# A conv and RWKV7 trunk step: the order planned by a detailed timing model, and solved columns transposed on chip

## The chip, the cores and the metric

One core of one Trainium2 chip runs the whole program. Its engines work side by side, each through its own instruction stream in a fixed order: TensorE (PE, matrix products into PSUM), VectorE (DVE), ScalarE (ACT), GpSimd (POOL) and SyncE (SP, which here only issues DMAs). An instruction waits in its stream until what it needs is there, and everything behind it on that engine waits with it. The metric is device time in microseconds for one launch; the kernel before was run three times, and its median counts.

## The reference, cut to what matters

A layer of width 1024 over one prompt of 2048 positions and 8 short samples. All columns are one projection of the normalised input, half of them go to a short convolution, half to an RWKV-7 recurrence of 8 heads of 64, and the concatenated results go through an output projection:

```python
p = xn @ w_in
u = cg * h;  z = conv_w[0]*u_ext[:, 0:T] + conv_w[1]*u_ext[:, 1:T+1] + conv_w[2]*u_ext[:, 2:T+2]
y_conv = bg * z * silu(gc)
# recurrence, per head:
sa = einsum('bhij,bhj->bhi', S, -kk_t)
S  = S * w_t + sa (kk_t a_t)^T + v_t k_t^T
o  = einsum('bhij,bhj->bhi', S, r_t)
y  = concatenate([y_conv, group_norm(o) ... * silu(gr)]) @ w_out
out = rms_norm(x + y)
```

## The kernel before

**Tiling.** The prompt is worked in two halves (hf) of 1024 positions, and each half in four pairs of heads (p), so there are eight passes, pairs 0 to 7. A half has three blocks of columns, 256 (330 with the samples in the first half), 384 and 384 wide. Every projection is a sum over 8 pieces of the depth and three products of high and low parts (xh*wh, xl*wh, xh*wl), 24 matmuls into one PSUM tile `pj`; of these there are two buffers.

**One pass.** `rwkv_pair` projects k, r, v and the gate of the pair and, block by block, makes the decays and the small matrices: `amat` multiplies `L` by `bk` into PSUM tiles `ax` (four or three chunks, two heads), DVE masks the result into `AB` and `L`, POOL scales `AB` by `Q`. When a block is done, `store_blocks` writes the two 32x32 diagonal blocks of every chunk's triangular matrix to DRAM (`dn`). `inverse` (L640) reads them back as `na`, one small matrix to a partition, and solves: `subst` takes 31 steps of two DVE operations each, `sub<-xi,na` and `xi<-xi,sub`. Its result `xi` has one small matrix to a partition; the matmuls that follow (`cx`, 32x32) need the matrix over 32 partitions, so `xi` goes to DRAM (`dx`, two DMAs, L669) and comes back in another order (twelve DMAs into `AB`, L678), and DVE transposes one copy into `na` (L680) for a product. After the `cx` products `AB` holds the full inverse.

`wkv` then carries the state through 16 chunks of 64 positions, strictly one after the other. A chunk of the two heads is twelve fp32 matmul instructions of 64 columns, and a chain runs through them: `ca<-sv,L` (PE), the copy `xs` (DVE, L741), `ca<-xs,AB` (PE), `u` (DVE, L751), `cb<-u,bt` (PE), and two scalar_tensor_tensor operations that make the next state `sv` (DVE, L120), from which the next chunk's `ca` starts. `oo` (the output) and `cb<-sv,bt` stand beside the chain. Projections of the next pair and of the convolution (`conv_group`) don't depend on it, and can stand between its links on PE.

At the end `out_weights` and 17 output tiles of 512-column projections follow.

**What sets the order.** The loops are written as above, pass by pass, but instructions aren't issued in that order: the framework's scheduler, inside `tile.TileContext` (L1020 of before), plans an order for each engine ahead of time, from the dependencies, the buffers and the times that it estimates. That order is fixed in the program. SP issues nearly all loads and stores in one queue of this kind.

Of the kernel before, what the change touches and what calls it, by code (L numbers as in the profile page):

```python
# [8 lines left out]
F32 = mybir.dt.float32  # L9
# [4 lines left out]
ALU = mybir.AluOpType  # L14
# [73 lines left out]
def trunk_kernel(ctx, tc, I, O):  # L88
    nc = tc.nc
# [9 lines left out]
    def T(pool, shape, tag, bufs=1, dt=F32):  # L99
        cnt[0] += 1  # L100
        return pools[pool].tile(shape, dt, tag=tag, bufs=bufs, name=f"{tag}_{cnt[0]}")
# [71 lines left out]
    pool.memset(ucarry, 0.0)  # L173

    def derive():
        dve.tensor_scalar(out=omm, in0=prm[:, P_MU:P_MU + 17], scalar1=-1.0, scalar2=1.0, op0=ALU.mult, op1=ALU.add)
        dve.tensor_scalar(out=nkk, in0=prm[:, P_KK:P_KK + 4], scalar1=-1.0, scalar2=None, op0=ALU.mult)
# [462 lines left out]
    def inverse(S):  # L640
# [5 lines left out]
        for q in range(2):  # L646
            pool.memset(xf[q * 64:q * 64 + 64, q::34], 1.0)
        for q in range(2):
            sync.dma_start(out=na[q * 64:q * 64 + 64], in_=S.dn.rearrange("h b c s t -> (h b c) s t"))
        if cb:  # L650
# [14 lines left out]
        yield  # L665
        cnt[0] += 1
        dx = dram.tile([2, 2, 16, 16, 2, 32], F32, tag="dx", bufs=2, name=f"dx_{cnt[0]}")
        for q in range(2):
            sync.dma_start(out=dx[:, :, :, :, q, :].rearrange("h b c s t -> (h b c) s t"), in_=x[q * 64:q * 64 + 64])  # L669
        ty = T("pair", [128, 2, 16, 32], "na", 1)  # L670
        t1, ys = ty[:, 0], ty[:, 1]
        for bl in S.bls:
            AB, n, c0_ = S.AB[bl.i], bl.nch, bl.ch0
            e = 1 if bl.samp else 0
            for h in range(2):
                for b in range(2):
                    r = h * 64 + b * 32
                    sync.dma_start(out=AB[r:r + 32, e:e + n, b * 32:b * 32 + 32],  # L678
                                   in_=dx[h, b, c0_:c0_ + n].rearrange("c s q t -> (s q) c t"))
            dve.transpose(out=t1[:, c0_:c0_ + n, :], in_=AB[:, e:e + n, 0:32])  # L680
            py = CX([128, n, 32])
            for c in range(n):
                for h in range(2):
                    a, b = h * 64, h * 64 + 32
                    mm(py[b:b + 32, c, :], AB[a:a + 32, e + c, 32:64], t1[a:a + 32, c0_ + c, :])
            copy(ys[32:64, c0_:c0_ + n], py[32:64])
# [342 lines left out]
```

## Time and profile before

| | before |
|---|---|
| median of three runs | 1621.16 us (1619.57 to 1629.75) |
| profiled execution, its own time | 1613.0 us |
| span in the profile | 1610.9 us |
| PE busy | 1512.1 us, 94% |
| DVE busy | 1011.3 us, 63% |
| ACT busy | 616.2 us, 38% |
| POOL busy | 289.6 us, 18% |
| mean granted clock of TensorE | 0.969 |

The span is the time from the first to the last instruction of the profiled execution, and its own time has what lies around it. Busy shares are averages over stages that differ: PE is full in some stretches and has holes in others, so the page is read first for who could be the bound, and the stretches are then looked at one by one. The granted clock is 1.00 at 2.4 GHz and 0.50 at 1.2 GHz; a mean between them says how long each held.

### The profile page before, as it was taken

To read this page: it belongs to the slowest core of one execution; us is meant where nothing else is said; L and a number is where in the kernel's file an instruction comes from. 1 tells how busy PE (TensorE), PEld (TensorE's weight loads), DVE (VectorE), ACT (ScalarE), POOL (GpSimd) and SP (SyncE) were. 2 spreads that over 40 slices of the span, in tenths; PEclk is the share of its full clock that TensorE was granted. 3 is DMA by queue.
4 is the path that set the end of the run, shared out by engine and by line. 5 is a ranking of instruction groups with operands and counts; after the bars stand their busy time and mean duration, and the time that the engine had idled before them with its cause. 6 is when DMAs were issued, how large, how long until landed. Compare 5 with 4: busy or idle time off the path is not lost.

```text
span 1610.9 us, 29335 instructions
## 1 busy us (share of the span) xinstructions
PE 1512.1 (94%) x11088; PEld 1265.4 (79%) x11088; DVE 1011.3 (63%) x3101; ACT 616.2 (38%) x1591; POOL 289.6 (18%) x395
## 2 busy tenths in 40 slices
PE   4999999999999999989999999999999999899997
PEld 4989778887788777877789678877897788567885
DVE  6377458765687458784586358545864578466544
ACT  6443346324542354344541354135313543342221
POOL 3134103311133112320022002200220022000000
PEclk9989999899999998999999899999999999899999
DMA  7323412342043213441124112411241145414441
GB/s 241 118 83 110 137 49 74 108 122 78 20 136 113 95 50 112 140 125 61 36 73 125 42 36 66 135 39 37 77 127 38 34 118 155 133 62 137 143 137 53
DMA packets 121967, 151.90 MB, mean 94 GB/s; under 512 B 62617, under 2 KB 86681, under 8 KB 121826
## 3 DMA queue, kind: packets, MB, share of 16 engines
q1 hardware_dynamic: 107024, 104.53, 21.2%
q0 software_dynamic: 9536, 34.64, 6.8%
q10 hardware_dynamic: 5266, 10.86, 1.9%
q8 instruction: 88, 1.44, 0.4%
q14 instruction: 53, 0.43, 0.1%
HBM read 92.60 MB, written 57.35 MB: 93 GB/s over the span
## 4 chain that ended last, share of the span: by engine, by line
PE 63%; DVE 23%; issue 5%; DMA 5%; ACT 2%; POOL 1%; SPq 1%; ACTq 0%; DVEq 0%; POOLq 0%
PE pj L129 41%; PE ca L129 5%; PE ax L129 5%; DVE sub L123 5%; PE cb L129 4%; DVE xi L123 4%; DVE hp L123 2%; PE oo L129 2%; PE cx L129 2%; DVE hp L120 1%; PE cx L703 1%; DVE bk L123 1%; DVE t L120 1%; DMA dx<-xi 1%; DMA AB<-dx 1%
## 5 line engine op out<-in xcount | busy, mean ns | idle before, releaser
L129 PE MATMUL pj<-xh,wh 128*128 128x384 f32 (+3 forms) x1856 | 655.4, 354 | 18.0 <-DVE hp L123 13.8
L129 PE MATMUL pj<-xl,wh 128*128 128x384 f32 (+3 forms) x1856 | 652.8, 352 | 2.7 <-POOL xl L207 2.1
L129 PE MATMUL pj<-xh,wl 128*128 128x384 f32 (+3 forms) x1856 | 650.9, 351 | 0.8 <-DMA wl<-wsp 0.8
L129 PEld LDWEIGHTS pj<-xh,wh 128*128 128x128 f32 x1856 | 356.7, 192 | 50.1 <-DVE hp L123 11.5
L129 PEld LDWEIGHTS pj<-xl,wh 128*128 128x128 f32 x1856 | 356.8, 192 | 31.7 <-POOL xl L207 3.0
L129 PEld LDWEIGHTS pj<-xh,wl 128*128 128x128 f32 x1856 | 355.8, 192 | 27.3 <-issue 1.7
L117 ACT ACTIVATE tS<-sv,wc 64x64 f32<-64x64 f32 x256 | 88.0, 344 | 114.8 <-DVE sv L120 94.2
L207 POOL TENSOR_TENSOR wl<-wr,wh 128x512 fp32r<-128x512 f32 x66 | 87.8, 1342 | 193.4 <-ACT wh L117 190.0
L120 DVE SCALAR_TENSOR_TENSOR sv<-cb,wc,tS 64x64 f32<-64x64 f32 x240 | 68.0, 283 | 62.6 <-PE cb L129 56.1
L129 PE MATMUL ax<-L,bk 64*128 64x128 f32 x528 | 79.1, 298 | 20.9 <-DVE bk L123 11.2
L129 PEld LDWEIGHTS ax<-L,bk 64*128 64x128 f32 x528 | 66.1, 197 | 37.9 <-issue 23.6
L123 DVE TENSOR_TENSOR sub<-xi,na 128x126 f32<-128x126 f32 (+22 forms) x248 | 81.5, 329 | 16.5 <-DMA na<-dn 9.7
L117 ACT ACTIVATE t<-pj,prm 128x384 f32<-128x384 f32 (+3 forms) x170 | 68.8, 433 | 54.5 <-PE pj L129 53.4
L751 DVE TENSOR_SCALAR u<-ca,Q 128x64 f32<-128x64 f32 x128 | 36.2, 283 | 82.3 <-PE ca L129 82.1
L531 POOL TENSOR_TENSOR bk<-t,t 64x384 f32<-64x384 f32 (+2 forms) x56 | 58.3, 1041 | 155.3 <-ACT t L503 72.9
L123 DVE TENSOR_TENSOR xi<-xi,sub 128x126 f32<-128x126 f32 (+22 forms) x248 | 77.6, 313 | 7.1
L117 ACT ACTIVATE wh<-wr 128x512 fp32r<-128x512 f32 x66 | 40.5, 626 | 92.0 <-PE pj L129 73.1
L129 PEld LDWEIGHTS ca<-sv,L 128*64 128x64 f32 x528 | 43.3, 134 | 37.2 <-DVE sv L120 12.8
L129 PE MATMUL ca<-sv,L 128*64 128x64 f32 x528 | 67.8, 245 | 0.1
L741 DVE COPY xs<-ca 128x64 f32<-128x64 f32 x128 | 28.7, 224 | 60.4 <-PE ca L129 50.6
L298 POOL DMA_DIRECT2D wh<-wsp x33 | 18.6, 565 | 254.1 <-PE pj L129 216.7
L123 DVE TENSOR_TENSOR hp<-pj,hp 128x512 f32<-128x512 f32 (+1 forms) x34 | 23.4, 689 | 62.6 <-PE pj L129 62.2
(207 smaller groups left out, 2057.4 us busy)
## 6 DMA issues: line engine op xcount, KB each, us to landing
wr<-in_w_in SPq DMA_DIRECT2D x66, 256.0 KB, 3.7
wsp<-wh SPq DMA_DIRECT2D x33, 512.0 KB, 3.1
wsp<-wl SPq DMA_DIRECT2D x33, 512.0 KB, 3.5
wh<-wsp POOLq DMA_DIRECT2D x33, 512.0 KB, 3.6
wl<-wsp POOLq DMA_DIRECT2D x33, 512.0 KB, 4.8
hp<-in_x_prompt SPq DMA_DIRECT2D x28, 512.0 KB, 4.1
la<-yd SPq DMA_DIRECT2D x16, 512.0 KB, 4.0
out_y_p<-hp ACTq DMA_DIRECT2D x16, 512.0 KB, 2.6
```

Source lines behind the costliest of these rows:

```text
L117: act.activation(out=out, in_=in_, func=AF.Copy, scale=scale, bias=bias)
L120: eng.scalar_tensor_tensor(out=out, in0=in0, scalar=scalar, in1=in1, op0=op0, op1=op1)
L123: dve.tensor_tensor(out=out, in0=in0, in1=in1, op=op)
L129: pe.matmul(out, lhsT=lhsT, rhs=rhs, start=start, stop=stop)
L207: eng.tensor_tensor(out=lo, in0=src, in1=hi.bitcast(F32), op=ALU.subtract)
L298: pool.dma_start(out=wh, in_=wsp[col, 0])
L531: pool.tensor_tensor(out=S.bk[bl.i][hs, chs, h, :], in0=ta[hs, a:a + n].rearrange("p (c j) -> p c j", j=64), in1=wi[hs, a:a + n].rearrange ...
L703: pe.transpose(out=pb[:, i, :], in_=S.bk[bi][:, ca + i].rearrange("p a t -> p (a t)"), identity=ident)
L741: dve.tensor_copy(out=xs_, in_=px)
L751: dve.tensor_scalar(out=u, in0=pu, scalar1=S.Q[:, q:q + 1], scalar2=None, op0=ALU.mult)
```

## The change

Two things change. The context is opened with `schedule_with_timeline_sim=True`, so the scheduler plans with a detailed timing model, and the instruction order of every engine comes out anew. And `inverse` turns its solved columns without DRAM: `na` is loaded so that the small matrices of a 32-partition group lie together (eight DMAs of 16 partitions), the ones of the start are set by a copy of a new constant `odd`, and after the substitution one DVE transposition of 32x32 squares over the whole of `xi` (128 partitions, 512 columns) is followed by twelve of 32 partitions that write `AB`; the tile of the first one, read with a stride, is the moving operand of the first `cx` product. The two DMAs to `dx`, the twelve from it and the three old transpositions fall away. The computation is the same.

```diff
--- before.py
+++ after.py
@@ -172,7 +172,11 @@
     ucarry = T("const", [128, 4, 2], "ucarry")
     pool.memset(ucarry, 0.0)
 
+    odd = T("const", [128, 2], "odd")
+
     def derive():
+        dve.tensor_reduce(out=odd, in_=ident.rearrange("p (g q c) -> p q g c", g=4, q=2), axis=mybir.AxisListType.XY,
+                          op=ALU.add)
         dve.tensor_scalar(out=omm, in0=prm[:, P_MU:P_MU + 17], scalar1=-1.0, scalar2=1.0, op0=ALU.mult, op1=ALU.add)
         dve.tensor_scalar(out=nkk, in0=prm[:, P_KK:P_KK + 4], scalar1=-1.0, scalar2=None, op0=ALU.mult)
         dve.tensor_scalar(out=hwa, in0=prm[:, P_W0:P_W0 + 8], scalar1=0.5, scalar2=None, op0=ALU.mult)
@@ -644,9 +648,11 @@
         pool.memset(x, 0.0)
         xf = x.rearrange("p c t -> p (c t)")
         for q in range(2):
-            pool.memset(xf[q * 64:q * 64 + 64, q::34], 1.0)
-        for q in range(2):
-            sync.dma_start(out=na[q * 64:q * 64 + 64], in_=S.dn.rearrange("h b c s t -> (h b c) s t"))
+            pool.tensor_copy(out=xf[:, q::34], in_=odd[:, q:q + 1].to_broadcast([128, 16]))
+        for g in range(4):
+            for q in range(2):
+                r = g * 32 + q * 16
+                sync.dma_start(out=na[r:r + 16], in_=S.dn[g // 2, g % 2])
         if cb:
             ab = S.AB[0][:, 0, 0:64]
             dd = T("small", [128, 8], "dd", 1)
@@ -663,26 +669,20 @@
                 bmask.unsqueeze(2).to_broadcast([128, 8, 8]))
         yield from subst(na, x, 32, 2)
         yield
-        cnt[0] += 1
-        dx = dram.tile([2, 2, 16, 16, 2, 32], F32, tag="dx", bufs=2, name=f"dx_{cnt[0]}")
-        for q in range(2):
-            sync.dma_start(out=dx[:, :, :, :, q, :].rearrange("h b c s t -> (h b c) s t"), in_=x[q * 64:q * 64 + 64])
-        ty = T("pair", [128, 2, 16, 32], "na", 1)
-        t1, ys = ty[:, 0], ty[:, 1]
+        ty = T("pair", [128, 2, 512], "na", 1)
+        dve.transpose(out=ty[:, 0], in_=xf)
+        z = ty[:, 0].rearrange("p (s c) -> p c s", c=16)
+        ys = ty[:, 1].rearrange("p (c t) -> p c t", t=32)
         for bl in S.bls:
             AB, n, c0_ = S.AB[bl.i], bl.nch, bl.ch0
             e = 1 if bl.samp else 0
-            for h in range(2):
-                for b in range(2):
-                    r = h * 64 + b * 32
-                    sync.dma_start(out=AB[r:r + 32, e:e + n, b * 32:b * 32 + 32],
-                                   in_=dx[h, b, c0_:c0_ + n].rearrange("c s q t -> (s q) c t"))
-            dve.transpose(out=t1[:, c0_:c0_ + n, :], in_=AB[:, e:e + n, 0:32])
+            for r in range(0, 128, 32):
+                dve.transpose(out=AB[r:r + 32, e:e + n, r % 64:r % 64 + 32], in_=z[r:r + 32, c0_:c0_ + n, :])
             py = CX([128, n, 32])
             for c in range(n):
                 for h in range(2):
                     a, b = h * 64, h * 64 + 32
-                    mm(py[b:b + 32, c, :], AB[a:a + 32, e + c, 32:64], t1[a:a + 32, c0_ + c, :])
+                    mm(py[b:b + 32, c, :], AB[a:a + 32, e + c, 32:64], z[a:a + 32, c0_ + c, :])
             copy(ys[32:64, c0_:c0_ + n], py[32:64])
             dve.tensor_copy(out=ys[96:128, c0_:c0_ + n], in_=py[96:128])
             pt = CX([128, n, 32])
@@ -1017,7 +1017,7 @@
         I[name] = nc.dram_tensor(f"in_{name}", a.shape, mybir.dt.from_np(a.dtype), kind="ExternalInput").ap()
     for name, shape in _OUTS:
         O[name] = nc.dram_tensor(f"out_{name}", shape, F32, kind="ExternalOutput").ap()
-    with tile.TileContext(nc) as tc:
+    with tile.TileContext(nc, schedule_with_timeline_sim=True) as tc:
         trunk_kernel(tc, I, O)
     r = run_bass_kernel_spmd(nc, [arrays], core_ids=[0])
     o = {name: r.results[0][f"out_{name}"].reshape(shape) for name, shape in _OUTS}
```

How the order moves shows best on PE in the recurrence. The first place runs from the end of pair 5's first chunk through its second; `ca`, `cb` and `oo` are the chunk's matmuls, `pj` projections of other work, `cx` transpositions for later chunks. Before:

```order
L129 MATMUL cb_11167<-u_11181,bt_11148 64x64 x2
L129 MATMUL oo_11165<-u_11181,AB_1738_10345 64x64 x2
L129 MATMUL pj_12171<-xh_1221_7515,wh_12107 128x384
L129 MATMUL pj_12171<-xl_1222_7516,wh_12107 128x384
L129 MATMUL ca_11166<-sv_11149,L_1732_10339 64x64
L129 MATMUL oo_11165<-sv_11149,L_1732_10339 64x64
L129 MATMUL ca_11166<-sv_11149,L_1735_10342 64x64
L129 MATMUL oo_11165<-sv_11149,L_1735_10342 64x64
L129 MATMUL cb_11167<-sv_11149,bt_11148 64x64 x2
L715 MATMUL cx_11239<-cst_90,v_1724_10331 128x128 x2
L129 MATMUL ca_11166<-xs_11193,AB_1738_10345 64x64 x2
L129 MATMUL pj_12171<-xh_1221_7515,wl_12108 128x384
```

In the new order, from the same point on:

```order
L129 MATMUL cb_11175<-u_11189,bt_11156 64x64 x2
L129 MATMUL oo_11173<-u_11189,AB_1734_10352 64x64 x2
L129 MATMUL ca_11174<-sv_11157,L_1728_10346 64x64
L129 MATMUL oo_11173<-sv_11157,L_1728_10346 64x64
L129 MATMUL ca_11174<-sv_11157,L_1731_10349 64x64
L129 MATMUL oo_11173<-sv_11157,L_1731_10349 64x64
L129 MATMUL cb_11175<-sv_11157,bt_11156 64x64 x2
L129 MATMUL ca_11174<-xs_11201,AB_1734_10352 64x64 x2
L129 MATMUL cb_11175<-u_11210,bt_11156 64x64 x2
L129 MATMUL oo_11173<-u_11210,AB_1734_10352 64x64 x2
```

Between the links of the chain the projections are gone; the chunks after this one look the same, up to the seventh.

The second place is the end of that pair's eighth chunk, on PE; `t`, `L_2017` and `bk_2026` in the second fence belong to the next pair's blocks, and `ax` is the PSUM tile of `amat`. Before:

```order
L129 MATMUL cb_11313<-u_11402,bt_11231 64x64 x2
L129 MATMUL oo_11310<-u_11402,AB_1739_10346 64x64 x2
L129 MATMUL pj_12262<-xh_1221_7515,wl_12199 128x384
L129 MATMUL pj_12262<-xh_1221_7515,wh_12198 128x384
L129 MATMUL ca_11410<-sv_11378,L_1733_10340 64x64
L129 MATMUL oo_11310<-sv_11378,L_1733_10340 64x64
L129 MATMUL ca_11410<-sv_11378,L_1736_10343 64x64
```

In the new order, from the same point on:

```order
L129 MATMUL cb_11321<-u_11410,bt_11239 64x64 x2
L129 MATMUL oo_11318<-u_11410,AB_1735_10353 64x64 x2
L703 MATMUL cx_11443<-cst_90,bk_1739_10357 128x128 x4
L129 MATMUL ax_12424<-cst_90,t_12413 128x2 x2
L129 MATMUL ax_12442<-L_2017_12101,bk_2026_12110 128x128 x4
L129 MATMUL pj_12498<-xh_1219_7520,wh_12297 128x384
L129 MATMUL pj_12498<-xl_1220_7521,wh_12297 128x384
L129 MATMUL pj_12498<-xh_1219_7520,wl_12298 128x384
L129 MATMUL pj_12498<-xh_1219_7520,wh_12297 128x384
L129 MATMUL pj_12498<-xl_1220_7521,wh_12297 128x384
L129 MATMUL ca_11418<-sv_11386,L_1729_10347 64x64
L129 MATMUL ca_11418<-sv_11386,L_1732_10350 64x64
```

The chunk's `cb` and `oo` and the next chunk's `ca` now have the next pair's `amat` between them, and right before the rows shown 18 projection matmuls stand in one run.

The third place is SP's queue around the inverse of pair 0. Before, with `wr` a weight load and `yd` stores of the convolution (the load of `na` stands eight rows further up, as two DMAs of 64x1024):

```order
L669 DMA dx_1277<-xi_1147 1024x1x32 x2
L384 DMA yd_84<-hp_2013 128x320
L303 DMA wr_113<-in_w_in 128x512
L384 DMA yd_85<-hp_2013 128x384
L678 DMA AB_85_377<-dx_1277 32x4x32 x4
L678 DMA AB_86_378<-dx_1277 32x6x32 x4
L678 DMA AB_87_379<-dx_1277 32x6x32 x4
L384 DMA yd_86<-hp_2013 128x384
```

In the new order, with `wsp` stores of split weights, from the last `dn` store on:

```order
L641 DMA dn_895<-AB_88_381 32x6x32 x4
L655 DMA na_1148<-dn_895 16x1024 x8
L388 DMA yd_84<-hp_2016 128x320
L309 DMA wsp<-wh_2450 128x1024
L310 DMA wsp<-wl_2451 128x1024
```

The round trip through `dx` is gone and `na` is loaded by eight DMAs. On DVE, right behind the last substitution step, stands in its place:

```order
L123 TENSOR_TENSOR sub_1279<-xi_1149,na_1148 128x30
L123 TENSOR_TENSOR xi_1149<-xi_1149,sub_1279 128x15x2
L123 TENSOR_TENSOR sub_1282<-xi_1149,na_1148 128x16
L123 TENSOR_TENSOR xi_1149<-xi_1149,sub_1282 128x16
L673 STREAM_TRANSPOSE na_1285<-xi_1149 128x512
L680 STREAM_TRANSPOSE AB_86_379<-na_1285 32x4x32 x4
L680 STREAM_TRANSPOSE AB_87_380<-na_1285 32x6x32 x4
L680 STREAM_TRANSPOSE AB_88_381<-na_1285 32x6x32 x4
L120 SCALAR_TENSOR_TENSOR hp_2419<-pj_2589,omm_97,t_2585 128x384
```

Thirteen transpositions follow each other without another operation between them.

## Rows read from the trace of the kernel before

**Rows 1.** The page: engines, and ax<-L,bk (busy, mean | idle before).

```profile
PE 1512.1 (94%) x11088; PEld 1265.4 (79%) x11088; DVE 1011.3 (63%) x3101; ACT 616.2 (38%) x1591; POOL 289.6 (18%) x395
...
L129 PE MATMUL ax<-L,bk 64*128 64x128 f32 x528 | 79.1, 298 | 20.9 <-DVE bk L123 11.2
```

**Rows 2.** Busy time by stretch: wkv of pair 5; sum over all eight.

```profile
1061.60:1120.70 59.10, 59.10 (x554) 44.02 (x552) 29.55 (x125) 24.93 (x77) 2.61 (x6) 1.00 0.13 43
...
sum 476.50, PE 476.50 PEld 346.75 DVE 262.16 ACT 221.20 POOL 19.27; mean PE 59.56 PEld 43.34 DVE 32.77 ACT 27.65 POOL 2.41
```

**Rows 3.** Busy time by stretch: sum over the seven stretches between.

```profile
sum 780.50, PE 716.84 PEld 645.04 DVE 546.10 ACT 277.86 POOL 208.97; mean PE 102.41 PEld 92.15 DVE 78.01 ACT 39.69 POOL 29.85
```

**Rows 4.** Timeline, one chunk of pair 5: start, us, engine, line, operation, [idle].

```profile
1063.03 0.33 PE L129 MATMUL cb<-u,bt 64*64 64x64 f32 x4
...
1063.41 0.60 DVE L120 SCALAR_TENSOR_TENSOR sv<-cb,wc,tS 64x64 f32<-64x64 f32 x2 [0.60 <-PE cb L129]
...
1063.95 0.38 PE L129 MATMUL ca<-sv,L 128*64 128x64 f32 x3
...
1064.48 0.22 DVE L741 COPY xs<-ca 128x64 f32<-128x64 f32 x1 [0.47 <-PE oo L129]
...
1064.70 0.44 PE L715 MATMUL cx<-cst,v 128*128 128x128 f32 x2
...
1065.07 0.33 PE L129 MATMUL ca<-xs,AB 64*64 64x64 f32 x4
...
1065.45 0.28 DVE L751 TENSOR_SCALAR u<-ca,Q 128x64 f32<-128x64 f32 x1 [0.74 <-PE ca L129]
...
1065.61 0.33 PE L129 MATMUL pj<-xh,wh 128*128 128x384 f32 x1
...
1065.78 0.34 PE L129 MATMUL pj<-xl,wh 128*128 128x384 f32 x1
```

**Rows 5.** Timeline, PE: one run of 256-column projection matmuls, with its edges.

```profile
1071.81 0.38 PE L129 MATMUL pj<-xh,wh 128*128 128x256 f32 x1
...
1072.03 0.28 PE L129 MATMUL pj<-xl,wh 128*128 128x256 f32 x1
...
1072.27 0.28 PE L129 MATMUL pj<-xh,wh 128*128 128x256 f32 x1
...
1072.48 0.33 PE L129 MATMUL cb<-u,bt 64*64 64x64 f32 x4
```

**Rows 6.** Waits: engine and line, awaited; us in total, times, longest.

```profile
PE cx L129 <- DVE na L680: 14.6, 6, 5.2
```

**Rows 7.** The chain that ended last, at pair 5's dx round trip.

```profile
1038.22 3.58 DMA dx<-xi
...
1042.72 3.57 DMA AB<-dx
...
1046.75 0.57 PE cx L129 x16
```

**Rows 8.** All of L680, the transpositions of before: ns min/median/max.

```profile
L680 DVE STREAM_TRANSPOSE na<-AB x24: 304/378/379, 174.5 to 1381.4; 128x192 f32<-128x192 f32 x16, 128x128 f32<-128x128 f32 x8
```

**Rows 9.** Timeline, SP: issue of eight of twelve AB<-dx DMAs.

```profile
1043.73 4.65 SPq L678 DMA_DIRECT2D AB<-dx  x8
```

**Rows 10.** Busy time by stretch; PEclk is the number after POOL's.

```profile
1376.40:1384.30 7.90, 3.76 (x112) 3.26 (x112) 2.23 (x7) 2.28 (x5) 0.00 (x0) 0.60 0.84 292
...
1044.10:1046.70 2.60, 0.00 (x0) 0.00 (x0) 0.31 (x1) 0.00 (x0) 0.00 (x0) 1.00 1.10 366
1046.90:1053.70 6.80, 6.80 (x70) 5.73 (x67) 1.44 (x5) 1.36 (x5) 0.00 (x0) 0.50 0.34 76
```

**Rows 11.** Timeline, PE, after a hole: 384-column projection matmuls.

```profile
163.01 0.69 PE L129 MATMUL pj<-xh,wh 128*128 128x384 f32 x1 [2.45 <-DVE hp L123]
163.50 0.52 PE L129 MATMUL pj<-xl,wh 128*128 128x384 f32 x1
163.82 0.52 PE L129 MATMUL pj<-xh,wl 128*128 128x384 f32 x1
```

## The prediction, made before the changed kernel was run

> **What bounds the kernel now.** I read the page first: in [rows 1] PE is busy 94% of the span of 1610.9 us, DVE 63%. So time can be won only as PE work that goes away, as PE idle time that goes away, or at the clock. I then cut the span into stages with the busy-time-by-stretch view. [Rows 2] are the eight recurrence stages (wkv): together 476.5 us in which PE is busy without a hole at clock 1.00 (that of pair 5 stands for them, 59.1 us for 16 chunks). [Rows 3] are the seven stretches between them: 780.5 us with PE busy 716.8, so the holes are here.
>
> To tell work from waiting I made a ledger: every matmul of the order times its spacing to the next in the timeline. A 384-column projection matmul (pj) is spaced 0.17 us (1065.61 to 1065.78) [rows 4], a 256-column one 0.12 (two of them from 1072.03 to 1072.27) [rows 5]. Of a chunk's 12 small fp32 instructions (the trace has two records for each) six take 0.75 us, from 1063.95 to 1064.70 [rows 4], so 0.12 each and 1.45 us a chunk. Summed over the whole order this gives 1456 us of PE work before, of which 472.5 in the wkv stages (the trace has 476.5: the ledger is good to 1%) and 680 in the seven stretches, so 780.5 - 680 = 100 us of stall there. The rest is the first 198 us, which I leave as it is, and the output projection.
>
> **The change, term by term.** The scheduling flag moves every engine's order; the two edits of inverse() are smaller.
>
> *Fewer, longer projection runs: -73 us.* Whenever PE goes from a small fp32 matmul to pj, or back, [rows 5] show an extra delay: the first of a run takes 0.22 (1071.81 to 1072.03) and the last 0.21 (1072.27 to 1072.48), where those between take 0.12. That is 0.10 at each end, 0.2 for a run. In the order of before (counted there, as in the new one) pj stand in 684 runs, in the new one in 318 (5568 pj in both): 366 x 0.2 = 73 us less PE work, 1383 in all. Nothing hides this, since PE is the bound.
>
> *Bare chunks in wkv: +123 us.* Before, two to five pj stand at several points in nearly every chunk. In the new order, 11 of 16 chunks of a pair have no pj between the links of the chain (six in a row, then five), and the fills stand in blocks of about 20 pj, with blocks 0 and 1 of the next pair inside them. A bare chunk then runs at its latency, from [rows 4]: cb to the first stt 0.38 (1063.03 to 1063.41), two stt 0.60, ca<-sv until xs may start about 0.35, xs 0.27 with its handoff, ca<-xs to u 0.38 (1065.07 to 1065.45), u and handoff 0.33: 2.3 us. PE's own work in it is 1.45, so about 0.9 us of PE stands still, 11 x 8 x 0.9 = 77 us. In the filled chunks the waits for xs, u and stt behind long blocks cost more. I added up each chunk at its three waits (the longer of what PE has queued, what DVE has queued, and the latency). For the order of before this gives 469.6 us, against 476.5 measured, 1.5% too little; for the new order it gives 641, so 651 with that correction, against 523 of PE work in these stages. That is 127.6 us of stall, against 476.5 - 472.5 = 4 before: +123. Bounds: 77 (the bare chunks alone) and 150.
>
> *Stalls between the wkv stages: -72 us.* Of the 100 us I put down to the dx round trip: the cx matmuls waited 14.6 us in all, six times, for the transposes that follow it [rows 6]. In pair 5 the chain shows dx<-xi for 3.58 us and AB<-dx for 3.57 us ahead of the first cx at 1046.75 [rows 7]. Behind such a hole the clock is at half for a while, there 0.50 from 1046.90 to 1053.70 [rows 10]; with pj spaced 0.32 instead of 0.17 in it that is some 3 us lost, at four pairs 12. Together 27 us. The new code replaces the trip by DVE work: one 128x512 and then 12 transposes of 32 partitions. [Rows 8] have 0.304 us for 128 columns and 0.378 for 192; the slope to 512 gives an estimate of 0.75, and four of at most 0.31 stand before the first cx, so 2.0 us instead of the 8.5 from 1038.22 to 1046.75 [rows 7]. All 13 are 0.75 + 4 x 0.31 + 8 x 0.38 = 5 us of DVE per pair, under PE's pj in this stretch (DVE is busy 546 of 780.5 us) [rows 3]. If that cover failed it would be 8 x 4 = 32 us. The load of na becomes 8 DMAs rather than two; eight of AB<-dx took SP 4.65 us to issue [rows 9], so six more put the last some 3 us later. That is covered by the same pj or costs up to 8 x 3 = 24 us; I take zero, because subst has PE work in front of it in the new order (52 us of it from the end of wkv to the first cx). The ones set by a copy on POOL cost nothing: POOL is busy 18% of the span [rows 1]. Of the other 73 us, mostly waits of ax<-L,bk for DVE and POOL in the three blocks (20.9 us right before it) [rows 1] and the half clock behind them, the new order takes two blocks of three into the wkv stage, where the sum above has priced them; I take 45. Together 72, between 27 (only dx) and 100.
>
> *The clock in bare chunks: +52 us.* [Rows 10] show what the clock does after PE had little to do: from 1044.10 to 1046.70 PE is busy 0.00, and the next 6.8 us are at 0.50, which is 1.2 GHz instead of 2.4; from 163.01, after 2.45 us without work, pj are spaced 0.32 instead of 0.17 [rows 11]. The wkv stage of [rows 2], like the other seven, stands at 1.00, and all of them carry pj. The bare chunks have PE at about 60%, with nothing but small matmuls, for 14 and 12 us on end, and no stretch of before is like that. The nearest row is 1376.40 to 1384.30, small matmuls of the cx stage with PE busy 3.76 of 7.90 us: clock 0.60 [rows 10]. By that I take the drop as likely. Its price lies between 0 and 0.9 us a chunk (all of the small matmuls on the chain doubled); I take 0.5 for some 8 of 11 chunks, 4 us a pair, and at each return to pj about ten of them at 0.32 rather than 0.17, 1.5 us, twice a pair: 7 us a pair, seven and a half pairs, 52. Bounds 0 and 90.
>
> The Trainium skill (TensorE: Matmul & The Clock Gate, Part 1, HAM oscillation — how this bites in real kernels) ties the loss of clock to long idle gaps of PE between bursts, while the section after it, A second HAM failure mode, has short, frequent idling do the same. By the first rule, gaps of under 1 us as in a bare chunk would leave the clock full and the sum would lack its last term; by the second it stands. The 0.60 row speaks for the second.
>
> *Sum.* -73 + 123 - 72 + 52 = +30. The profiled execution took 1613.0 us (span 1610.9), so 1643 on its scale. The median of the runs is 1621.2, 8 above the profiled one: 1651 against it, +1.8%.
>
> **Rivals.**
> (a) *The clock stays full in the bare chunks.* For it: each gap in them is short, and all of wkv was at 1.00 so far; against it: the 0.60 row. The last term goes: 1651 - 52 = 1599, 1.4% faster than before. It decides on the other side at a single place, the eleven bare chunks of each pair, and turns where the clock costs 73 - 123 + 72 = 22 us, 3 us a pair.
> (b) *The waits in wkv are smaller than added up.* If only the bare chunks cost and the filled ones run as before, 77 stands for 123: 1605; with the low end of the third term as well, 45 less gain: 1650. Between them, about 1620, no change that can be told. For it: the formula fits the old order, where waits are few, and has not been tried on one with long fills.
> (c) *The blocks of the next pair stall the chain.* In the new order ax<-L,bk stand in PE's queue between two links of the recurrence (the second place shown with the change). Each waits for DVE and POOL, and behind it wait ca, u and the state. At 2 to 3 us for two such places a pair: 8 x 5 = 40 more, 1691. Before, such waits stood outside the chain.
> (d) *The inverse part alone counts*, and the new order is as good as the old one: 1621 - 27 = 1594. The 684 against 318 runs and the bare chunks speak against it.
>
> **How the numbers follow.** A measurement of this kernel tells about 1% from no change (1605 to 1637). Forecast, 1625 to 1680: 0.46. (a), 0.18, ends under 1605 in two of three cases. (b), 0.20, half within 1%, a quarter on each side. (c), 0.12, slower. (d), 0.04, faster. Faster 0.12 + 0.05 + 0.04 = 0.21; within 1%: 0.06 of (a), 0.10 of (b), 0.07 of the forecast's low end = 0.23; slower 0.39 + 0.05 + 0.12 = 0.56. The range reaches from (d), 1594, to (c), 1691; the forecast's own is 1625 to 1680.
>
> **What would show it.** Right: wkv stages of 70 to 85 us where they took 57 to 65; u in them about 2.3 to 3 us apart in two rows of chunks and 8 us or more at three or four places; the granted clock at 0.50 inside wkv; no PE idle before the first cx of more than a microsecond, and the stretches between at 85 to 95 us. Wrong: wkv stages at clock 1.00 (then (a)), stages under 65 us (then (b)), ax<-L,bk waiting over 2 us inside wkv (then (c)), or the first cx still behind a wait, now for na<-dn or the transposes, which would take the 27 us back.

## The result

The changed kernel takes 1770.9 us (median of four runs, 1769.4 to 1773.5) against 1620.4 us before: 1.092 times as long, 95% interval 1.087 to 1.097. The direction was forecast, at a chance of 0.56, the size was not: 1651 was predicted, the range ended at 1691, and the loss is 150 us, not 30. The profiled execution of the changed kernel has a span of 1771.7 us, 160.8 more than before.

The page of the kernel after, first the engines' busy time, then the granted clock in 40 slices:

```profile
PE 1588.5 (90%) x11088; PEld 1363.6 (77%) x11088; DVE 1051.8 (59%) x3182; ACT 618.0 (35%) x1591; POOL 291.1 (16%) x395
...
PEclk9999877997699867989679976997799689996879
```

PE is busy 76 us longer than in [rows 1] although it runs the same 11088 matmuls: it spends more of its time at half clock. The mean granted clock is 0.872 where it was 0.969.

The same cut into stages as in [rows 2] and [rows 3], for the kernel after: the wkv stage of pair 5 and the sum of all eight, by stretch (the number after POOL's is the granted clock):

```profile
1190.80:1279.00 88.20, 79.30 (x600) 63.82 (x598) 50.37 (x166) 35.28 (x96) 9.67 (x17) 0.73 0.11 31
...
sum 764.80, PE 685.47 PEld 545.37 DVE 436.27 ACT 287.30 POOL 77.73; mean PE 85.68 PEld 68.17 DVE 54.53 ACT 35.91 POOL 9.72
```

And the seven stretches between them (first a pair of the first half, then one of the second, then the sum):

```profile
315.40:420.20 104.80, 93.86 (x665) 85.59 (x665) 61.35 (x174) 33.49 (x89) 27.33 (x29) 0.94 0.34 111
...
1108.30:1190.80 82.50, 80.72 (x625) 77.03 (x623) 52.42 (x155) 22.19 (x62) 16.54 (x25) 1.00 0.30 95
...
sum 711.20, PE 661.87 PEld 603.97 DVE 459.19 ACT 227.72 POOL 150.16; mean PE 94.55 PEld 86.28 DVE 65.60 ACT 32.53 POOL 21.45
```

And start and end (the last row is a part of the end):

```profile
0.00:221.60 221.60, 193.02 (x1237) 178.63 (x1237) 125.19 (x305) 90.28 (x210) 63.26 (x87) 0.96 0.39 131
1697.60:1771.70 74.10, 48.15 (x198) 35.60 (x195) 31.19 (x114) 12.68 (x29) 0.00 (x0) 0.82 0.20 64
1700.40:1720.80 20.40, 6.34 (x15) 4.40 (x16) 6.83 (x28) 3.15 (x7) 0.00 (x0) 0.50 0.32 100
```

The prediction's ledger gives the work in each of them (the matmuls of the order at full clock and their spacings). What is left of the time is called stall, so the 160.8 us can be put down to stages:

| | work before | time before | work after | time after | change in stall |
|---|---|---|---|---|---|
| eight wkv stages | 472.5 | 476.5 | 523.4 | 764.8 | +237 |
| seven stretches between | 680 | 780.5 | 638 | 711.2 | -27 |
| start, to the first cb | 158.8 | 198.2 | 177.8 | 221.6 | +4 |
| end, behind the last cb | 144.9 | 155.7 | 44.2 | 74.1 | +19 |

With the 73 us less of PE work that makes 161, as it must, since stall is whatever the ledger leaves. The forecast for the four lines was +175, -72, 0 and 0.

### The profile page after: what moved, and what is told of

It is laid out like the page before. It is cut to its first block, busy times and chain, and to the rows that moved or that the text cites. A ratio compares the mean times of both kernels' runs of the same rounds, so it can differ in the third digit from the quotient of the medians.

```text
span 1771.7 us, 29155 instructions
## 1 busy us (share of the span) xinstructions
PE 1588.5 (90%) x11088; PEld 1363.6 (77%) x11088; DVE 1051.8 (59%) x3182; ACT 618.0 (35%) x1591; POOL 291.1 (16%) x395
## 4 chain that ended last, share of the span: by engine, by line
PE 68%; DVE 19%; issue 5%; DMA 4%; ACT 3%; POOL 1%; SPq 1%; DVEq 0%; POOLq 0%; ACTq 0%
PE pj L129 46%; PE ax L129 6%; PE ca L129 5%; PE cb L129 4%; PE oo L129 2%; DVE sub L123 2%; DVE xi L123 2%; DVE c L120 2%; PE cx L129 2%; DVE hp L120 2%; DVE sv L120 1%; DVE u L751 1%; PE cx L703 1%; DVE hp L123 1%; DVE AB L680 1%
## 5 line engine op out<-in xcount | busy, mean ns | idle before, releaser
L129 PEld LDWEIGHTS pj<-xh,wh 128*128 128x128 f32 x1856 | 367.5, 198 | 77.0 <-DVE t L120 12.9
L129 PEld LDWEIGHTS pj<-xl,wh 128*128 128x128 f32 x1856 | 367.8, 198 | 22.6 <-DVE xl L211 2.6
L129 PEld LDWEIGHTS pj<-xh,wl 128*128 128x128 f32 x1856 | 365.7, 197 | 18.8
L117 ACT ACTIVATE t<-pj,prm 128x384 f32<-128x384 f32 (+3 forms) x170 | 67.6, 435 | 160.8 <-PE pj L129 160.4
L129 PE MATMUL ca<-sv,L 128*64 128x64 f32 x528 | 87.9, 300 | 27.8 <-DVE sv L120 21.9
L129 PEld LDWEIGHTS ca<-sv,L 128*64 128x64 f32 x528 | 57.1, 174 | 59.0 <-DVE sv L120 37.9
L123 DVE TENSOR_TENSOR sub<-xi,na 128x126 f32<-128x126 f32 (+22 forms) x248 | 69.6, 281 | 41.4 <-DMA na<-dn 35.4
L123 DVE TENSOR_TENSOR AB<-ax,msk 64x384 f32<-64x384 f32 (+2 forms) x88 | 48.8, 554 | 55.2 <-PE ax L129 54.1
L129 PE MATMUL cb<-u,bt 64*64 64x64 f32 x512 | 52.3, 292 | 29.7 <-DVE u L751 29.2
L129 PE MATMUL oo<-sv,L 128*64 128x64 f32 x528 | 75.9, 278 | 0.0
L129 PEld LDWEIGHTS cb<-u,bt 64*64 64x64 f32 x512 | 31.3, 167 | 56.7 <-DVE u L751 46.4
```

Source lines behind the costliest of these rows:

```text
L117: act.activation(out=out, in_=in_, func=AF.Copy, scale=scale, bias=bias)
L123: dve.tensor_tensor(out=out, in0=in0, in1=in1, op=op)
L129: pe.matmul(out, lhsT=lhsT, rhs=rhs, start=start, stop=stop)
```

## The experiments

Each was planned anew and timed beside the kernel before on its chip. The question was which part of the change makes the loss, and what in the wkv stages does it: the waits of a chain with nothing beside it, or the clock.

**The two parts alone.** First the new planning with the old inverse:

```diff
-    with tile.TileContext(nc) as tc:
+    with tile.TileContext(nc, schedule_with_timeline_sim=True) as tc:
```

> The new planning alone, with the old inverse (dx round trip). Theory A, the new order makes the loss and the inverse part only helps a little: 1771 plus the 27 us of the dx round trip, 1785 to 1800, with wkv stages of 84 to 95 us and the clock at 0.50 in them as in the changed kernel. Rival B, the two parts need each other (the transpositions put 5 us of DVE work per pair into a place where the new order has no cover): 1620 to 1700.

Measured: 1770.3 us, 1.095 times the kernel before (1.090 to 1.100). Its wkv stage of pair 5, by stretch:

```profile
1184.70:1275.10 90.40, 81.42 (x624) 66.19 (x622) 50.28 (x165) 36.42 (x99) 9.66 (x17) 0.77 0.10 31
```

It has nearly the clock of the changed kernel (0.77 against 0.73) and 90.4 us for 88.2. So the plan makes the whole loss, and theory A was right in that. But its 1785 to 1800 didn't come: the 27 us that the inverse part was to bring aren't there. Under this plan the round trip, still in place here, costs PE next to nothing at the first cx (waits of PE: awaited, total us, times, longest):

```profile
PE cx L129 <- DVE na L680: 0.3, 1, 0.3
```

Nor are the 27 us there in the converse, the inverse part under the old plan:

> The inverse part alone, planned as before. Theory A: the 14.6 us that cx waited and the half clock behind it go, 1590 to 1600, all wkv stages at clock 1.00 and 57 to 65 us. Rival B: the DVE transpositions or the eight loads of na take the place of the round trip, 1615 to 1630.

Measured: 1618.7 us, ratio 1.002 (0.998 to 1.006), no difference that can be told. Theory A is out. Rival B's time came, but not as it was put: in pair 5 cx starts 0.8 us behind the end of the substitution, so the transpositions cost little. PE waits at the first cx 14.3 us in all, as long as before (14.6 in [rows 6]), but in other pairs. Here are the waits of PE in pairs 0 to 3 of this kernel, in its pairs 4 to 7, and in pairs 4 to 7 of the kernel before:

```profile
PE cx L129 <- DVE na L673: 10.7, 4, 5.2
...
PE cx L129 <- DVE na L673: 3.5, 3, 1.4
...
PE cx L129 <- DVE na L680: 14.4, 5, 5.2
```

In pairs 0 to 3 the kernel before waits 0.2 us. So the waits went in the second half and came up in the first. A first suspect for what took the gain was a place on DVE, here the timeline of pair 5 from the last mask on:

```profile
1043.29 0.55 DVE L123 TENSOR_TENSOR L<-ax,msk 64x384 f32<-64x384 f32 x1
...
1048.18 0.55 DVE L123 TENSOR_TENSOR hp<-hp,pj 128x384 f32<-128x384 f32 x1 [3.40 <-PE pj L129]
...
1059.47 0.56 DVE L123 TENSOR_TENSOR hp<-hp,pj 128x384 f32<-128x384 f32 x1 [3.76 <-PE pj L129]
1059.94 0.18 DVE L123 TENSOR_TENSOR sub<-xi,na 128x31 f32<-128x31 f32 x1
```

and on SP in the same place:

```profile
1045.80 4.79 SPq L655 DMA_DIRECT2D na<-dn  x8
```

The eight loads of na take 4.8 us to issue (two took 1.1 before), and in this plan the substitution (sub at 1059.94) stands behind five products hp<-hp,pj of the convolution, which wait for PE; before, two stood there. The substitution begins 16 us after the mask, where it began 11 us after it. In this pair, though, PE waits at cx less than before, 1.05 us for 2.71.

**Whether that place can be mended.** The loads split between two queues:

```diff
-            for q in range(2):
+            for q, eng in enumerate((sync, act)):
                 r = g * 32 + q * 16
-                sync.dma_start(out=na[r:r + 16], in_=S.dn[g // 2, g % 2])
+                eng.dma_start(out=na[r:r + 16], in_=S.dn[g // 2, g % 2])
```

> The inverse part alone under the old plan, with the eight loads of na issued four on SP and four on ACT. With all eight on SP, the substitution of a pair stood behind five convolution products in DVE's planned order (two before the change) and began 16 to 19 us after the last mask instead of 9 to 11; in this plan three stand before it in most pairs. Theory F, the planner's late place for the substitution eats what the missing round trip gives: the start comes 2 to 4 us earlier in each pair and the whole at 1590 to 1608. Rival G, it is the transpositions or the cx products that eat it: no change against the inverse part alone, 1615 to 1625.

Measured: 1643.1 us, 1.016 (1.013 to 1.019), slower than either theory. The substitution did begin earlier, 10 us after the mask, and that didn't help; what made the kernel slower isn't shown. The four loads on ACT don't hold that engine here, although the profile names the store to dn behind its longest wait in this place (timeline of ACT in pair 5, then the same instruction in the kernel with all eight loads on SP):

```profile
1040.06 0.51 ACT L117 ACTIVATE hp<-hp,prm 128x256 f32<-128x256 f32 x1 [8.45 <-DMA dn<-AB]
```

```profile
1044.82 0.51 ACT L117 ACTIVATE hp<-hp,prm 128x256 f32<-128x256 f32 x1 [8.25 <-DVE hp L123]
```

In both it follows the product hp<-hp,pj of DVE, which ended at 1040.02 and at 1044.78.

The other way, dn stored twice by SP (dn has one more axis, q, for the copy), so that two DMAs load na:

```diff
+                for q in range(2):
+                    sync.dma_start(out=S.dn[h, b, q, bl.ch0:bl.ch0 + bl.nch].rearrange("c s t -> s c t"),
+                                   in_=S.AB[bl.i][r:r + 32, e:e + bl.nch, b * 32:b * 32 + 32])
...
+        for h in range(2):
+            sync.dma_start(out=na[h * 64:h * 64 + 64], in_=S.dn[h].rearrange("b q c s t -> (b q c) s t"))
```

> The inverse part alone under the old plan, with dn stored twice (eight stores a block instead of four) so that na comes back in two DMAs on SP as before the change. The plan then puts the substitution behind as few convolution products as before the change (two in pairs 4 to 6, where the eight loads had five). Theory F, the eight loads and the place that the planner gives the substitution for them ate the gain of the missing round trip: the substitution starts 9 to 12 us after the last mask, cx 8 us earlier than in the kernel before, and the whole at 1590 to 1605. Rival G: 1612 to 1625, no change.

Measured: 1636.9 us, 1.011 (1.006 to 1.015), again slower than both said. Here the start and the short path came that theory F named: in pair 5 the substitution begins 12 us after the mask, and cx comes 0.8 us after its end, where it was 9. Yet the stretch of pair 5 takes 100.3 us where it took 99.2. PE has the same 90 us of work in it: the plan now has less of it behind the masks and more before them (from the end of wkv to the last mask 49.7 us instead of 43.0), so cx comes no earlier, and PE waits for it no less, over all pairs (waits of PE):

```profile
PE cx L129 <- DVE na L672: 16.4, 7, 4.9
```

The profiled execution took 1651.4 us, 14.5 more than the median, and the clock is one place in it where time is lost. Pairs 4 to 6 have the same planned order in wkv, so these stretches (wkv of pairs 4, 5 and 6, and 23.6 us near the start of 5) show its price by itself:

```profile
925.50:985.70 60.20, 60.20 (x549) 43.64 (x548) 29.45 (x125) 24.48 (x77) 2.64 (x6) 1.00 0.14 42
1086.00:1156.70 70.70, 70.70 (x549) 50.32 (x547) 29.38 (x124) 24.55 (x77) 2.64 (x6) 0.81 0.11 35
1256.60:1316.80 60.20, 60.20 (x549) 43.63 (x548) 29.44 (x125) 24.48 (x77) 2.64 (x6) 1.00 0.14 42
1087.40:1111.00 23.60, 23.60 (x133) 16.01 (x133) 6.48 (x30) 5.65 (x17) 0.00 (x0) 0.50 0.00 1
```

In pair 5 the clock stayed at 0.50 through these 23.6 us, with PE busy all the time; by the stage's mean of 0.81 some 27 of its 70.7 us were at half, and it took 10.5 us more than its two likes. Just ahead of it, at 1084.46, PE had waited 1.82 us, which it did ahead of neither of the others. Why the median lies 14 us above the kernel before isn't settled by this trace; that the gain is absent is.

Last, the inverse part where it had shown a gain, in pairs 4 to 7:

```diff
-        run(inverse(S))
+        run((inverse if hf else inverse_dram)(S))
```

> The inverse part under the old plan in the second half of the prompt alone (pairs 4 to 7); pairs 0 to 3 keep the round trip through DRAM, and their order is that of the kernel before. In the kernel with the inverse part everywhere, pairs 5 to 7 stood 16 us less between their wkv stages than before the change, while the first half and pair 4 stood 42 us more. Theory H: the gain is real where PE idles at the first cx, and is lost where it did not (in the first half cx waits for nothing before the change): 1595 to 1610. Rival I, whatever stands there is only moved, and the stretches are set by PE's work and by the clock behind the cx products: 1613 to 1625.

Measured: 1601.8 us, 0.986 (0.982 to 0.990), as theory H said: 24 us faster than the kernel before on its chip (1625.7), and faster than the changed one. In pairs 4 to 7 the substitution still begins 16 to 18 us after the mask, behind five products, so in these pairs that place isn't what took the gain. PE waits at their first cx 3.9 us where it waited 14.4 (waits of PE):

```profile
PE cx L129 <- DVE na L730: 3.9, 3, 1.5
```

In the first half cx waited 0.2 us before the change, and the new inverse, which puts it right behind the substitution, makes it wait, here pair 1 of the kernel with the inverse part alone (timeline of PE):

```profile
355.54 0.64 PE L129 MATMUL cx<-na,AB 32*32 32x32 f32 x16 [5.24 <-DVE na L673]
```

By the ledger the stretches of pairs 4 to 7 lose 20 us of stall in this kernel (50 to 30). The three kernels with the new inverse in all pairs lose time in the other half: from the last u of a pair to the first of the next, pairs 1 to 3 take 410.7 us (inverse part alone), 407.4 (loads on two queues) and 390.4 (dn twice) where the kernel before takes 373.5, and pairs 4 to 7 take 416.8, 415.2 and 419.9 for 421.2. Part of that is work that the plan moves between stages. The kernel with dn stored twice is longer in its wkv stages too, 483.6 us for 460.2 from first to last u, 10.5 of it by the clock of pair 5.

**What the loss in wkv is.** In the changed kernel I gave PE something to do in the bare chunks that nobody needs, to see what the clock is worth. One matmul stands behind ca<-xs, one behind oo<-u:

```diff
+            fill = sample is None and q - cb in (1, 2, 3, 4, 5, 6, 8, 9, 10, 11, 12, 13)
+            if fill:
+                mm(pc[0][0:64, 4:6], xs_, cst[:, C_ID:C_ID + 128])
...
+            if fill:
+                mm(pc[0][0:64, 6:8], u, cst[:, C_ID:C_ID + 128])
```

> The changed kernel with two idle matmuls of 128 columns added to chunks 2 to 7 and 9 to 14 of every pair, one reading xs and one reading u, into an unused part of the ca bank; nothing reads them. They stand where PE waits for u and for the new state, so they need no time of the chain, about 0.2 us each of PE's idle time. Theory C, the half clock is what most of the loss is: the wkv stages go to clock 1.00 or nearly so, from 84 to 95 us down to 72 to 80, and the whole to 1660 to 1690. Rival W, the waits of the chain make the loss and the half clock only goes with them: the stages stay within 3 us, 1755 or more, since work was only added.

Measured: 1781.0 us, 1.102 (1.097 to 1.106). The test was spoiled in two ways. First, u waited for the first filler. DVE's timeline shows it, first with the filler, then the same place of the changed kernel:

```profile
1205.56 0.28 DVE L754 TENSOR_SCALAR u<-ca,Q 128x64 f32<-128x64 f32 x1 [0.79 <-PE ca L129]
```

```profile
1197.39 0.28 DVE L751 TENSOR_SCALAR u<-ca,Q 128x64 f32<-128x64 f32 x1 [0.43 <-PE ca L129]
```

DVE stood idle 0.79 us before u instead of 0.43, so a bare chunk took 2.8 us at full clock. This wait is the program's: ca<-xs and the filler write one PSUM tile, in different columns, and by the trace the semaphore that u waits for is raised by the filler, where in the changed kernel ca<-xs raises it. Second, the planner moved other work too: between the first and the last u of pairs 0 to 2 stand 166 projection matmuls, in the changed kernel 110. The second form has one filler of 256 columns behind oo<-u:

```diff
+            if sample is None and q - cb in (1, 2, 3, 4, 5, 6, 8, 9, 10, 11, 12, 13):
+                mm(pc[0][0:64, 4:8], u, cst[:, 0:256])
```

> The changed kernel with one idle matmul of 256 columns in chunks 2 to 7 and 9 to 14 of every pair, reading u and placed behind oo<-u, where PE waits 0.44 us for the new state; the matmul needs about that much, and the filler on xs that u had to wait for is gone. Theory C: the bare chunks take 2.4 to 2.6 us at clock 1.00 instead of 3.0 to 3.3 at 0.50, the long chunks behind them are shorter by 2 to 4 us, and the whole goes to 1670 to 1720. Rival W, the long chunks and their waits are the loss: bare chunks may be shorter, but the whole stays above 1740.

Measured: 1753.6 us, 1.085 (1.081 to 1.089), 17 us below the changed kernel, which ran on another chip; the intervals of the two ratios overlap. By its number that is rival W, but it decides little. The clock was held in part only (0.916 in the mean), the filler isn't free when it drops, as the next two show, and the plan came out otherwise: pair 5's stage holds 164 projection matmuls between its first and last u, in the changed kernel 115.

To have the bare chunk alone, I took the projections out of the chain under the old plan: the last convolution projection of a pair may only be issued behind the pair's last chunk.

```diff
+                    with (tc.issue_after(hold[-1]) if hold else nullcontext()):
                         mm(ps, wh[:, k, :], xh[:, k, :], start=(k == 0), stop=False)
```

> The kernel before with the last convolution projection of each pair (72 matmuls; not pair 3) planned behind the pair's last chunk. The old planner then leaves all 16 chunks of seven pairs without any projection, and no block of the next pair stands in them either: bare chunks alone, under the old plan, with no work added. By the trace of the changed kernel a bare chunk takes 2.45 us at clock 1.00 and 3.0 to 3.3 at 0.50. Theory C, the clock falls to 0.50 soon after the chunks go bare: wkv stages of 48 to 54 us, about 25 us of PE standing still in each, and the whole, with some 70 us less of run edges, at 1690 to 1750. Rival L, bare chunks cost their latency alone: stages of 38 to 42 us at 1.00, the whole at 1640 to 1680.

Measured: 1916.6 us, 1.186 (1.182 to 1.191). One wkv stage of it by stretch:

```profile
1246.30:1301.50 55.20, 45.45 (x400) 32.57 (x399) 26.42 (x118) 20.63 (x62) 0.46 (x2) 0.50 0.02 7
```

The stage takes 55.2 us at 0.50 with 25.2 us of work and no projection in it. That is nearly as long as the 59.1 us in [rows 2], which held some 150 projections more: they cost 4 us. And there was a second loss that I had not put in either number, the cover of the substitution (timeline of PE, first cx of pair 5):

```profile
1232.61 0.64 PE L131 MATMUL cx<-na,AB 32*32 32x32 f32 x16 [16.43 <-DVE na L683]
```

16.4 us of idle PE for 2.7. Then the same kernel with the filler of 256 columns in every bare chunk:

> The kernel with seven wkv stages of bare chunks under the old plan, and in each of their chunks one idle matmul of 256 columns behind oo<-u that reads u; the planned order is otherwise the same, so the clock is the only thing that should differ. Theory C: the stages go from 0.50 to 1.00 and from 55.2 us to 46 to 49, a bare chunk from 2.95 to 2.45 us, the projections behind the stage start at full clock, and the whole comes down from 1917 by 7 x 8 to 11, to 1840 to 1860. Rival L, the clock costs next to nothing in a chain that waits anyway: 1905 or more.

Measured: 1961.4 us, 1.203 (1.194 to 1.211); the whole went up, into rival L's range. In some stages the clock rose, in others not, which gives both prices in one trace (pairs 4 and 5, by stretch):

```profile
1079.80:1101.50 21.70, 18.13 (x193) 11.98 (x193) 12.36 (x56) 8.72 (x25) 0.00 (x0) 0.89 0.01 2
1278.00:1341.30 63.30, 56.07 (x430) 36.14 (x429) 26.38 (x118) 20.64 (x62) 0.47 (x2) 0.50 0.02 6
```

u in pair 4, at 1.00 (timeline of DVE):

```profile
1083.41 0.28 DVE L757 TENSOR_SCALAR u<-ca,Q 128x64 f32<-128x64 f32 x1 [0.70 <-PE ca L131]
...
1085.88 0.28 DVE L757 TENSOR_SCALAR u<-ca,Q 128x64 f32<-128x64 f32 x1 [0.43 <-PE ca L131]
```

and in the kernel without filler, at 0.50:

```profile
1251.34 0.28 DVE L757 TENSOR_SCALAR u<-ca,Q 128x64 f32<-128x64 f32 x1 [0.58 <-PE ca L131]
...
1254.26 0.28 DVE L757 TENSOR_SCALAR u<-ca,Q 128x64 f32<-128x64 f32 x1 [0.58 <-PE ca L131]
```

So a bare chunk takes 2.47 us at 1.00 and 2.92 at 0.50; with the filler it is 3.4 at 0.50 (the stage of 63.3 us). The clock is worth 0.45 us of a bare chunk, 15%, against 10.5 of 27 us, 39%, in the chunks of the kernel with dn stored twice, which hold projections. Theory C is right in the rows and wrong in the sum: the filler held the clock through no stage here, and it cost more where it failed than it brought where it held.

Last, the free projections put back between the links, under the new plan: one convolution projection of each pair (not of pair 3), three matmuls behind each ca<-xs and each oo<-u of chunks 2 to 7 and 9 to 14.

```diff
+                    with (tc.issue_after(hold[min((bl.i * KT + k) // 1, len(hold) - 1)]) if hold else nullcontext()):
```

> The changed kernel with one convolution projection of each pair (72 matmuls; not in pair 3) held back in the plan: three of its matmuls may not be issued before a given link of the chain, so every chunk that was bare has three to six projection matmuls again. Nothing else is changed, no work added. Theory D, the plan spends the free projections between the stages and leaves none for the chain: wkv stages of 60 to 72 us at clock 1.00, and the whole at 1620 to 1660. Rival E, what is put into the chain is missing in the stretches between, where the waits for blocks and the substitution then stand open: those stretches grow by 8 to 12 us a pair and the whole stays at 1720 or more.

Measured: 1958.0 us, 1.209 (1.205 to 1.214): rival E, and more than it said. The wkv stages did become shorter (72 to 83 us without pair 3's), but what the chain got the substitution lacked. Timeline of PE at the first cx of pair 6:

```profile
1467.69 0.65 PE L131 MATMUL cx<-na,AB 32*32 32x32 f32 x16 [29.11 <-DVE na L676]
```

29.1 us of idle PE, where the changed kernel has none, and the half clock behind it reaches through the first six chunks although they hold projections again (3.2 to 6.3 us each at 0.50).

## Why the prediction was right in direction and wrong in size

The sum was +30, and the traces differ by 161. Of the four terms that failed, the stretches between are the largest: -72 forecast, -27 measured. The clock is about 90 for 52 and the waits in wkv about 147 for 123, both estimates, and the end is +19 where nothing was put. That the direction came out rests on the two wkv terms, whose mechanism was right.

**Bare chunks: right mechanism, a little small.** DVE's timeline of pair 5 in the changed kernel:

```profile
1192.53 0.28 DVE L751 TENSOR_SCALAR u<-ca,Q 128x64 f32<-128x64 f32 x1 [1.50 <-PE ca L129]
...
1194.92 0.28 DVE L751 TENSOR_SCALAR u<-ca,Q 128x64 f32<-128x64 f32 x1 [0.43 <-PE ca L129]
...
1197.39 0.28 DVE L751 TENSOR_SCALAR u<-ca,Q 128x64 f32<-128x64 f32 x1 [0.43 <-PE ca L129]
...
1200.15 0.28 DVE L751 TENSOR_SCALAR u<-ca,Q 128x64 f32<-128x64 f32 x1 [0.58 <-PE ca L129]
...
1203.49 0.28 DVE L751 TENSOR_SCALAR u<-ca,Q 128x64 f32<-128x64 f32 x1 [0.42 <-PE ca L129]
```

u comes 2.39 and 2.47 us apart; 2.3 had been added up from [rows 4]. With the clock at half it is 3.0 to 3.3, but the clock isn't all of that: DVE also has the group norm of finished chunks there, and with that a chunk of the kernel with the 256-column filler takes 3.3 us at 1.00 (u at 1367.56 and 1370.90). The long chunks are there too, 14.1 us at the eighth, 12.3 and 14.1 at the end. PE hardly waits in them; the eighth by stretch:

```profile
1214.80:1228.90 14.10, 13.96 (x86) 12.13 (x87) 9.27 (x23) 6.33 (x20) 3.61 (x6) 0.85 0.24 75
```

They are long by the projections and blocks in PE's own queue and by the clock. Rival (c), that PE waits in the next pair's blocks, did not come: by the page PE idles 2.0 us before ax<-L,bk in the whole program (busy, mean | idle before):

```profile
L129 PE MATMUL ax<-L,bk 64*128 64x128 f32 x528 | 85.2, 293 | 2.0 <-DVE L L123 1.9
```

In the eight stages PE idles 79 us in all (764.8 less 685.5), 60 of them in chunks with fewer than ten projection or ax matmuls.

**The clock: right that it falls, too small by two fifths.** By stretch, the third chunk of pair 5 and what follows:

```profile
1196.20:1198.60 2.40, 1.68 (x25) 1.25 (x25) 1.01 (x5) 0.62 (x3) 0.00 (x0) 0.99 0.00 0
1199.20:1218.40 19.20, 16.02 (x123) 12.28 (x123) 13.44 (x54) 8.74 (x27) 1.34 (x3) 0.50 0.02 8
1219.10:1236.00 16.90, 15.85 (x129) 13.07 (x127) 7.95 (x25) 7.44 (x18) 2.85 (x5) 1.00 0.41 129
1236.20:1263.30 27.10, 24.15 (x157) 19.37 (x158) 19.02 (x63) 9.79 (x28) 2.80 (x5) 0.50 0.03 8
```

46 of the stage's 88 us are at 0.50; over the eight stages, from their clocks, some 360 us, of which 143 lie in chunks with ten or more projection or ax matmuls. I had priced eight bare chunks and two times ten projections a pair, about 30 us at half. The long chunks at half were missing: the fifteenth chunk's 12.3 us stand at 0.50 as a whole. With the two prices from the experiments, 39% of the 143 us and 15% of the other 220, that is about 90 in all, an estimate, for my 52. The rest of the 237, some 147, goes to the waits by subtraction, for my 123; the formula's 118 at full clock lies below that. The trace shows 79 us of it as idle PE, so the division between clock and waits stays an estimate.

In the bare chunks of pair 5, no wait of PE is over 0.39 us before the clock falls at 1198.6 to 1199.2 (timeline of PE):

```profile
1195.26 0.33 PE L129 MATMUL cb<-u,bt 64*64 64x64 f32 x4 [0.39 <-DVE u L751]
...
1196.04 0.33 PE L129 MATMUL ca<-sv,L 128*64 128x64 f32 x2 [0.33 <-DVE sv L120]
```

The prediction weighed two rules of the Trainium skill (TensorE: Matmul & The Clock Gate, Part 1). The trace agrees with the section A second HAM failure mode, where short, frequent idling loses the clock; the rule that only long gaps count would have given rival (a), which did not come.

**The stretches between: failed in two steps.** In the second half the step came out: the stall of pairs 4 to 7 went from 50 to 12 us, with the clock at 1.00, in pair 7's stretch at 0.97. But 27 us were put down to the missing dx round trip, and the two runs of the parts show that leaving it out in all pairs was worth nothing under either plan; here the new plan alone had taken the wait at cx away (0.3 us with the old inverse). In the first half the stall rose from 50 to 61: there every stage begins with the samples' chunk, a chain like the others, which the new plan leaves bare as well. By stretch, the place ahead of pair 1's stage, after and before:

```profile
406.40:420.20 13.80, 8.58 (x65) 4.71 (x63) 4.41 (x11) 5.27 (x19) 0.00 (x0) 0.63 0.06 20
```

```profile
358.00:371.40 13.40, 13.40 (x110) 9.96 (x108) 5.68 (x12) 6.44 (x22) 2.52 (x2) 1.00 0.24 83
```

PE idles 5.2 us there where it idled not at all, and it ends at half clock. I had counted it as a stretch between and not as a bare chain.

**The end: left out.** I took start and end as they were. In the new order only 192 projection matmuls are left behind the last chunk where there were 633, and the last group norm, the store of its result and the load for the output tiles, which those had covered, stand open. Timeline of PE:

```profile
1704.71 0.47 PE L866 MATMUL cx<-cst,c 128*128 128x128 f32 x1 [7.05 <-ACT c L860]
...
1715.89 0.79 PE L129 MATMUL pj<-xh,wh 128*128 128x512 f32 x1 [9.38 <-ACT wh L117]
```

16.4 us of waiting, at 0.50 (1700.40 to 1720.80 above), 19 us in all.

**Fewer runs: -73 us.** The 684 and 318 runs are what the traces have, but the 0.2 us a run are carried over from [rows 5]. The ledger holds them as an assumption, and no run tested them.

**Transpositions: right that they are hidden, a little small.** All instructions of the two lines in the changed kernel:

```profile
L673 DVE STREAM_TRANSPOSE na<-xi x8: 711/712/712, 180.3 to 1514.8; 128x512 f32<-128x512 f32 x8
```

```profile
L680 DVE STREAM_TRANSPOSE AB<-na x96: 367/495/515, 181.0 to 1521.7; 32x192 f32<-32x192 f32 x64, 32x128 f32<-32x128 f32 x32
```

0.71 us for the one of 512 columns (0.75 estimated), but those of 32 partitions take 0.37 to 0.52 where I took the 0.31 and 0.38 of 128 partitions: 6.3 us a pair for 5.

What stays open: how the 237 us of the wkv stages divide exactly between waits and clock, why the kernels with the loads on two queues and with dn stored twice are slower than the kernel before, and whether a plan with the projections spread and the substitution covered as well would be faster than both; after_hold shows that the one was bought with the other.

## What to carry to other kernels

Work that is free to be placed can cover one place only: before pricing a new order, look at who gets the free projections (the chain, the substitution, the end) and price each place that goes without, at half clock, not only the one that the change was about. A chain of short dependent steps with nothing beside it loses twice, by its latency and by the clock of what follows it. A shorter path to an instruction pays only where the engine waits at that instruction; elsewhere the new order can put a wait there, so test such a change stage by stage: here it was 24 us where it was made in the second half alone, and nothing where it was made in all pairs.

## What the hardware showed that was not expected

- The clock stayed at 0.50 for 23.6 us while PE was busy the whole time with the chain and the projections in it (pair 5 of the kernel with dn stored twice).
- The clock fell to 0.50 in chunks in which PE waited no longer than 0.39 us at a time (pair 5 of the changed kernel).
- A transposition by DVE of 32 partitions takes longer than one of 128 partitions with the same columns (0.37 to 0.52 us for the 0.30 to 0.38 of [rows 8]; source and target are strided here).
